# Queueing four kinds of loads behind the last tile's transposed exponentials in a two-layer decoder trunk

## The chip, the cores and the metric

One core of a Trainium2 chip runs the whole program. The metric is the device time of one execution in microseconds. PE is the matrix engine (TensorE), PEld its weight loads, DVE is VectorE, ACT is ScalarE, POOL is GpSimd, and SP is SyncE, whose queue issues every DMA of this kernel.

## The reference

Two layers of a decoder. The first is forgetting attention, the second a dilated sliding-window attention in three groups; both end in a gate and an output projection. The change touches only the first layer:

```python
def fox_mixer(h, w_in, b_f, q_g, k_g):
    proj = h @ w_in                                   # 1024 x 4112
    q = rms_norm(proj[..., :INNER]...); k = rms_norm(...); v = ...; gate = ...
    c = jnp.cumsum(jax.nn.log_sigmoid(f_logit), axis=1)
    o = fox_attention(q, k, v, c)     # softmax(q k / 8 + c_i - c_j, causal) v, 16 heads of 64
    return o.reshape(B, S, INNER), gate

x = x + (o * jax.nn.silu(gate)) @ w_out               # 1024 tokens, width 1024
```

## The kernel before, in words

Sequence and width are 1024 each. Products that need float32 accuracy run as three matmuls over a high and a low half of each operand. The heads are taken in eight pairs. For each pair a loop goes over eight tiles of 128 tokens: PE projects keys, queries and values of the tile (line 313, 24 matmuls), and between these matmuls PE works on the attention of pairs that were projected earlier. The classes and functions that matter:

- `Weights.load(i)` (line 253) brings quarter i of the next pair's raw weights, 384 KB, into one of two buffers called `raw`. `bound(i)` (line 258) reduces it on DVE to `vm`, and `split(k)` makes the high half on ACT (line 289) and the low half on POOL or DVE (line 291). A buffer is free when its two splits are done.
- `heads_tile`, `heads_sums` and `heads_pair` normalize the projected heads. ACT squares the projection into `sq` (line 383), DVE sums the squares (line 396) and scales (lines 398, 419, 420, 422), and the result is split into `hl` on ACT, POOL and DVE (lines 424 to 426). `turn()` (line 430) has a transposing DMA write two tiles' keys and queries to `qk_t`.
- `load_bc(hp, h, es)` (line 624) broadcasts half h of the cumulative forget sums of a head, 256 KB, to `bc`.
- `fox_tile(hp, t, ...)` is the attention of one tile of 128 queries. Its `score(e, c)` has PE make scores `s` in PSUM for head e of the pair (line 450, and the diagonal mask at line 656; three such PSUM buffers), and DVE adds `bc`, takes the running maximum and writes `p` (line 658), which frees the PSUM buffer. `p_transpose` then takes the exponential on ACT (line 492), splits it into the two halves of `ph` on ACT (line 495) and POOL (line 498), and one transposing DMA turns `ph` into `ptt` (line 499). There are two `ph` buffers, so a cast into `ph` waits until the transpose two places earlier has landed. `values(e)` has PE multiply `ptt` by the values `vt` (lines 506 to 508) into `o`; DVE divides (lines 688, 691), and the result goes to `y_d` (line 695). `gsf` (line 640) is the gate of the tile.

A counter called `Flow` runs four ticks per tile, and every step is queued at a tick. Tile 7's scores of a pair are due 57 and 59 ticks after the pair begins, and its values 67 and 69 ticks after. A pair takes 32 ticks, so while PE projects pair q it still finishes tile 7 of pair q-2. PE's own order is the written one. On the other engines and on the SP queue a scheduler decides the order at build time: it lets an instruction go ahead of one written earlier if it expects it to be ready sooner, and nothing but data and buffers holds it back. Each engine and the SP queue then take their instructions strictly in that order.

Of the kernel before, what the change touches and what calls it, by code (L numbers as in the profile page):

```python
# [2 lines left out]

# [1 line left out]

# [17 lines left out]
P = 128  # L23
# [3 lines left out]
NT = S // P  # L27
NH = 16
HD = 64
NHP = NH // 2  # L30
# [52 lines left out]
def trunk(ctx, tc, ins, out, cfg):  # L83
    nc = tc.nc
# [20 lines left out]
    flow = Flow()  # L105

    layer = {}

    def next_layer(bufs):
        if layer:  # L110
# [16 lines left out]
    c_d = dram.tile([NH, S], F32, name="c_d")  # L127
# [110 lines left out]
    class Weights:  # L238
# [9 lines left out]
        def load(self, i, tag=None):  # L248
            if tag is None:
                self.raw[i] = w_p.tile([P, 2, 384], F32, name="raw", tag="raw", bufs=2)  # L250
            else:
                self.raw[i] = lay([P, 2, 384], F32, name="raw", tag=tag)
            nc.sync.dma_start(self.raw[i][:, :, : self.n], self.src[:, 2 * i : 2 * i + 2, :])

        def bound(self, i):
            if self.vcols is None:
# [230 lines left out]
    def p_transpose(ne, nk, exps, splits):  # L487

        ph = lay([P, ne, 2, nk], F16, name="ph", tag="ph")
        pt = lay([P, ne * 2 * nk // P, P], F16, name="ptt", tag="ptt")  # L490
        for p, acc in exps:
            nc.scalar.activation(p, p, AF.Exp, bias=acc, scale=-1.0)  # L492
        for e, cols, p, pool_l in splits:
            if cfg["ph"]:
                nc.scalar.copy(ph[:, e, 0, cols], p)  # L495
            else:
                nc.vector.tensor_copy(ph[:, e, 0, cols], p)
            (nc.gpsimd if pool_l else nc.vector).tensor_sub(ph[:, e, 1, cols], p, ph[:, e, 0, cols])  # L498
        nc.sync.dma_start_transpose(pt, ph.rearrange("p e a k -> p (e a k)"))
        return pt.rearrange("p (e a k) s -> p e a k s", a=2, e=ne)  # L500

    def pv(o, e, blocks, vt):
# [116 lines left out]
    bcs = {}  # L619

    def load_bc(hp, h, es=(0, 1)):
        for e in es:
            bcs[hp, e, h] = lay([P, 512], F32, name="bc", tag="ga")
            nc.sync.dma_start(bcs[hp, e, h], c_d[2 * hp + e, h * 512 : (h + 1) * 512].partition_broadcast(P))

    def fox_tile(hp, t, kts, vt, sl):
        LP = cfg["lpf"]
        nk = (t + 1) * P
        st = {}
        pieces = [(a, min(a + 512, nk)) for a in range(0, nk, 512)]  # L630
        both = len(pieces) == 1
        accs = {}
        ptl = {}
        ps = {0: [], 1: []}

        def score(e, c):
            a, b = pieces[c]
            if e == 0 and c == 0:
                gs = st["gs"] = lay([P, P], F32, name="gsf", tag="gsl")
                nc.sync.dma_start(gs, gs_d[t * P : (t + 1) * P, hp * P : (hp + 1) * P])  # L640
            if c == 0:
                accs[e] = BIG
                st["acc"] = sm.tile([P, 2], F32, name="acc", tag="acc", bufs=8)
            if t < 2:
                if e == 0:
                    st["p"] = lay([P, 2, nk], F32, name="p", tag="p")
                p = st["p"][:, e]
            else:
                p = lay([P, b - a], F32, name="p", tag="p")
            ps[e].append(p)  # L650
            s = ps_s.tile([P, 512], F32, name="s", tag="s")
            runs = [(kts[j // 2], j % 2, n) for j, n in key_runs(range(a // P, b // P))]
            scores(s, kts[t // 2], t % 2, e, runs, b < nk)
            if b == nk:

                nc.tensor.matmul(s[:, t * P - a : b - a], ident_b, tri_b, start=False, stop=True, skip_group_check=True)
            acc = st["acc"][:, c : c + 1]
            nc.vector.tensor_tensor_reduce(p, s[:, : b - a], bcs[hp, e, a // 512][:, : b - a], -1.0, accs[e], ALU.add, ALU.min, acc)  # L658
            accs[e] = acc
            pl = (cfg["pl"] & 1, cfg["pl"] >> 1 & 1)  # L660
            if c < len(pieces) - 1 or both and e == 0:
                return
            if both:
                exps = [(ps[i][0], accs[i]) for i in range(2)]
                if t < 2:
                    splits = [(slice(0, 2), slice(0, nk), st["p"], pl[1])]
                else:
                    splits = [(i, slice(0, nk), ps[i][0], pl[i]) for i in range(2)]
                pt = p_transpose(2, nk, exps, splits)
                for i in range(2):  # L670
                    ptl[i] = [(pt[:, i, 0, j], pt[:, i, 1, j], j) for j in range(t + 1)]
            else:
                exps = [(p, accs[e]) for p in ps[e]]
                splits = [(0, slice(*pieces[i]), ps[e][i], pl[i]) for i in range(2)]
                pt = p_transpose(1, nk, exps, splits)
                ptl[e] = [(pt[:, 0, 0, j], pt[:, 0, 1, j], j) for j in range(t + 1)]

        def values(e):
            if e == 0:
                st["o"] = ps_o.tile([P, 2, HD + 1], F32, name="o", tag="o")  # L680
            pv(st["o"], e, ptl[e], vt)
            if e == 1:
                finish()

        def finish():
            o = st["o"]
            rec = sm.tile([P, 2], F32, name="rec", tag="rec")
            nc.vector.reciprocal(rec, o[:, :, HD])
            y = sb.tile([P, P], F32, name="y", tag="y")
            for e in range(2):  # L690
                nc.vector.scalar_tensor_tensor(y[:, e * HD : (e + 1) * HD], o[:, e, :HD], rec[:, e : e + 1], st["gs"][:, e * HD : (e + 1) * HD], ALU.mult, ALU.mult)
            if hp == NHP - 1:
                turn_last(y, t, flow.now + 3)
            else:
                nc.sync.dma_start(y_d[t * P : (t + 1) * P, hp * P : (hp + 1) * P], y)


        ts, tv = cfg["fox"][both]
        for e in range(2):
            for c in range(len(pieces)):  # L700
                urgent(lambda e=e, c=c: score(e, c), "ps", sl + ts[e * len(pieces) + c])
            urgent(lambda e=e: values(e), "pv", sl + LP + tv[e])
# [29 lines left out]
    for hp in range(NHP):  # L732
        w2 = (fox_weights(hp + 1) if hp + 1 < NHP else part(w_fo, 0)).ahead()
        s0 = flow.now
        if hp == 0:
            load_bc(0, 0)
# [3 lines left out]
        kts = []  # L740
# [3 lines left out]
        for t in range(NT):  # L744
# [4 lines left out]
            if t % 2:  # L749
                with tc.high_priority(cfg["ph_"]):  # L750

                    turn = heads_pair(0, t - 1, hd)
                    flow.at(flow.now + (6 if hp < NHP - 1 else 4), lambda turn=turn, kts=kts: kts.append(turn()))
                for i in range(2):

                    tt = t - 1 + i
                    fox_tile(hp, tt, kts, vt, s0 + (cfg["due"][tt] if hp < NHP - 1 else 4 * tt + 18))
            if hp == NHP - 1:

                a = max(flow.now + 1, s0 + cfg["due"][t] - 4 * NT + cfg["lpf"] + 9)  # L760
# [350 lines left out]
```

## Time and profile before

| what | value |
|---|---|
| median of 3 runs | 1816.11 us (1810.0 to 1819.2) |
| the profiled execution | 1818.5 us, its span 1816.7 us |
| mean granted PE clock | 0.99 |
| PE, PEld busy | 1737.0 us (96%), 1641.7 us (90%) |
| DVE, ACT, POOL busy | 1093.3, 1011.0, 973.5 us |
| DMA queue of SP | 288.36 MB, 71.4% of the 16 engines' span |

The times in the views are microseconds from the start of the span. The first layer's attention over the pairs lies between about 110 and 590 us; pairs 2 to 7 begin near 193, 247, 302, 357, 412 and 467 us. A matmul's busy time includes its latency, so a busy PE is not a PE at its peak; an idle PE, on the other hand, is a loss wherever nothing else makes up for it.

### The profile page before, as it was taken

The page shows a single profiled execution, that of the slowest core. Times are in us where ns is not written, and L with a number is a line of the kernel's source. Part 1 is how long each engine was busy: PE and PEld are TensorE (multiplying, and loading weights), DVE is VectorE, ACT ScalarE, POOL GpSimd, SP SyncE. Part 2 cuts the span into 40 slices and gives each one's busy share as a digit, 9 for nine tenths or more (in the row PEclk, how much of TensorE's full clock was granted, in tenths as well). Part 3 has the DMA queues.
Part 4 walks back from the last instruction along what each step waited for, and adds up shares of the span by engine and source line. Part 5 has one row for each costly group of instructions (what it writes and reads, how often), then busy time and mean ns, then how long its engine had stood idle before and what let it go on. Part 6 is the DMA issues. An engine that isn't in the chain of part 4 may idle for free.

```text
span 1816.7 us, 38150 instructions
## 1 busy us (share of the span) xinstructions
PE 1737.0 (96%) x13276; PEld 1641.7 (90%) x13276; DVE 1093.3 (60%) x3674; ACT 1011.0 (56%) x2696; POOL 973.5 (54%) x1175
## 2 busy tenths in 40 slices
PE   7999999999988989999999999999999999999999
PEld 6999888888876779999999989999999999999877
DVE  8546666666664453365556585666675666667631
ACT  6536666666665465455555665555555555555620
POOL 4215565556545431255656566667576666757530
PEclk9999999999999999999999999999999999999999
DMA  8447999999999763456767687667677776667852
GB/s 285 127 130 140 193 190 185 176 177 183 187 190 207 213 188 114 127 113 134 142 133 144 146 191 143 157 140 152 138 163 144 162 151 143 149 140 179 189 154 85
DMA packets 653189, 290.79 MB, mean 160 GB/s; under 512 B 512306, under 2 KB 616754, under 8 KB 652996
## 3 DMA queue, kind: packets, MB, share of 16 engines
q1 hardware_dynamic: 652996, 288.36, 71.4%
q8 instruction: 104, 1.70, 0.4%
q14 instruction: 89, 0.73, 0.1%
HBM read 126.46 MB, written 37.03 MB: 90 GB/s over the span
## 4 chain that ended last, share of the span: by engine, by line
PE 45%; DMA 12%; DVE 6%; ACT 4%; issue 3%; POOL 3%; SPq 1%; DVEq 0%; POOLq 0%; ACTq 0%
PE pj L313 33%; PE pj L336 7%; DMA raw<-in_w_dsw 5%; PE s L450 2%; DMA qk_t<-hl 2%; DMA ptt<-ph 2%; DMA og_d<-og 1%; POOL hl L425 1%; POOL w L291 1%; DMA cmb<-og_d 1%; DVE w L291 1%; DVE hl L426 1%; DVE u L422 1%; PE ob L506 1%; DVE p L906 1%
## 5 line engine op out<-in xcount | busy, mean ns | idle before, releaser
L313 PE MATMUL pj<-w,xh 128*128 128x384 f32 (+2 forms) x4864 | 1259.6, 341 | 30.2 <-ACT w L289 7.3
L313 PEld LDWEIGHTS pj<-w,xh 128*128 128x128 f32 x4864 | 873.1, 191 | 38.9 <-DVE ge L481 7.8
L313 PE MATMUL pj<-w,xl 128*128 128x384 f32 (+2 forms) x2432 | 817.6, 336 | 0.2 <-DVE xl L530 0.2
L313 PEld LDWEIGHTS pj<-w,xl 128*128 128x128 f32 x2432 | 464.7, 191 | 0.9 <-DVE xl L530 0.9
L291 POOL TENSOR_TENSOR w<-raw,w 128x384 fp32r<-128x384 f32 (+2 forms) x258 | 261.7, 1035 | 233.3 <-ACT w L289 228.8
L498 POOL TENSOR_TENSOR ph<-p,ph 128x512 f16<-128x512 f32 (+3 forms) x176 | 172.9, 999 | 161.9 <-ACT ph L495 160.7
L289 ACT CAST w<-raw 128x384 fp32r<-128x384 f32 (+2 forms) x352 | 162.6, 501 | 114.8 <-PE pj L336 37.4
L425 POOL TENSOR_TENSOR hl<-u,hl 128x512 f16<-128x512 f32 x128 | 151.2, 1181 | 125.0 <-ACT hl L424 124.9
L912 POOL TENSOR_TENSOR ph<-p,ph 128x768 f16<-128x768 f32 (+2 forms) x96 | 155.3, 1618 | 102.9 <-ACT ph L911 102.9
L383 ACT ACTIVATE sq<-pj 128x256 f32<-128x256 f32 x256 | 97.2, 380 | 168.9 <-DVE u L378 167.2
L450 PE MATMUL s<-qk_t 128*128 128x128 f16 (+1 forms) x1504 | 162.0, 248 | 19.2 <-DVE acc L658 10.4
L336 PE MATMUL pj<-xh,w 128*128 128x512 f32 x512 | 170.4, 404 | 2.2 <-ACT p L907 1.1
L258 DVE TENSOR_REDUCE vm<-raw 128x1 f32<-128x256 f32 x128 | 53.6, 419 | 156.2 <-DMA raw<-in_w_dsw 118.6
L506 PEld LDWEIGHTS <-ptt 128*128 128x128 f16 x1136 | 102.9, 98 | 48.8 <-issue 27.5
L389 DVE SCALAR_TENSOR_TENSOR vt<-pj,vsr,vt 128x128 f16<-128x128 f32 x256 | 89.6, 350 | 93.2 <-ACT vt L388 92.8
L450 PEld LDWEIGHTS <-qk_t 128*128 128x128 f16 x1504 | 110.2, 98 | 36.1 <-issue 22.0
L424 ACT CAST hl<-u 128x512 f16<-128x512 f32 x128 | 79.2, 619 | 104.9 <-DVE u L422 88.6
L495 ACT CAST ph<-p 128x512 f16<-128x512 f32 (+3 forms) x176 | 88.9, 537 | 72.7 <-DMA ptt<-ph 72.3
L492 ACT ACTIVATE p<-p,acc 128x512 f32<-128x512 f32 (+2 forms) x192 | 109.0, 609 | 30.6 <-DVE acc L658 27.4
L336 PEld LDWEIGHTS pj<-xh,w 128*128 128x128 f32 x512 | 97.6, 191 | 24.5 <-DVE xr L779 1.5
L378 DVE TENSOR_TENSOR u<-pj,gr 128x256 f32<-128x256 f32 x256 | 106.4, 416 | 18.4 <-PE pj L313 18.3
L907 ACT ACTIVATE p<-p,og 128x128 f32<-128x128 f32 (+1 forms) x256 | 98.1, 441 | 33.6 <-DVE og L906 33.4
(171 smaller groups left out, 2609.4 us busy)
## 6 DMA issues: line engine op xcount, KB each, us to landing
raw<-in_w_dsw SPq DMA_DIRECT2D x96, 384.0 KB, 3.7
raw<-in_w_fox SPq DMA_DIRECT2D x32, 384.0 KB, 3.7
og_d<-og SPq DMA_DIRECT2D x64, 132.0 KB, 3.2
cmb<-og_d SPq DMA_DIRECT2D x64, 132.0 KB, 3.3
bc<-c_d SPq DMA_DIRECT2D x32, 256.0 KB, 3.9
gs_d<-ge SPq DMA_DIRECT2D x32, 192.0 KB, 3.2
xt<-in_xt SPq DMA_DIRECT2D x16, 256.0 KB, 6.1
xrow<-in_x SPq DMA_DIRECT2D x8, 512.0 KB, 6.3
```

Source lines behind the costliest of these rows:

```text
L289: nc.scalar.copy(w[:, 0, :n], raw[:, k % 2, :n])
L291: eng.tensor_sub(w[:, 1, :n], raw[:, k % 2, :n], w[:, 0, :n].bitcast(F32))
L313: nc.tensor.matmul(ps[:, :n], a[:, k, cols], w.slabs[k][:, j, :n], start=(k == 0 and i == 0), stop=(k == KT - 1 and i == 2))
L336: nc.tensor.matmul(ps[m], w.slabs[k][:, j, m * P : (m + 1) * P], a[:, k, 512 * b : 512 * (b + 1)], start=(k == 0 and x == 0), stop=(k == K ...
L378: nc.vector.tensor_mul(u[:, t % 2].rearrange("p (a b) d -> p a b d", a=2), ps[:, : 4 * HD].rearrange("p (a b d) -> p a b d", a=2, b=2), gr ...
L425: nc.gpsimd.tensor_sub(hl[:, :, :4, 1], u, hl[:, :, :4, 0])
L450: nc.tensor.matmul(s[:, c0 : c0 + cnt * P].rearrange("p (c s) -> p c s", c=cnt), qk[:, i, blk], kk[:, j : j + cnt, e], start=(h == 0), sto ...
L492: nc.scalar.activation(p, p, AF.Exp, bias=acc, scale=-1.0)
L498: (nc.gpsimd if pool_l else nc.vector).tensor_sub(ph[:, e, 1, cols], p, ph[:, e, 0, cols])
L506: nc.tensor.matmul(o[:, e, :], hi, vt[:, j, e, HD:], start=(b == 0), stop=False, skip_group_check=True)
L907: nc.scalar.activation(p[:, e], p[:, e], AF.Exp, bias=acc[:, e : e + 1], scale=-1.0)
L912: nc.gpsimd.tensor_sub(ph[:, 1], st["p"], ph[:, 0])
```

## The change

A function `queued()` gives a context in which everything that is issued on SP is ordered behind one remembered instruction: the transposing DMA of tile 7's second head, of the pair that last traced it. The edge is one of issue order alone; nothing waits for that DMA to end. Three things are put in such a context: the loads of `bc` for the first half of the keys, the transposing DMA of tiles 6 and 7's keys, and quarter 0 of every raw weight load. No instruction is added or removed.

```diff
+    last = {}
+
+    def queued():
+        return tc.issue_after(last["late"]) if "late" in last else nullcontext()
...
         def load(self, i, tag=None):
...
-            nc.sync.dma_start(self.raw[i][:, :, : self.n], self.src[:, 2 * i : 2 * i + 2, :])
+            with queued() if i == 0 else nullcontext():
+                nc.sync.dma_start(self.raw[i][:, :, : self.n], self.src[:, 2 * i : 2 * i + 2, :])
...
     def p_transpose(ne, nk, exps, splits):
...
-        nc.sync.dma_start_transpose(pt, ph.rearrange("p e a k -> p (e a k)"))
+        last["ptt"] = nc.sync.dma_start_transpose(pt, ph.rearrange("p e a k -> p (e a k)")).ins
...
     def load_bc(hp, h, es=(0, 1)):
         for e in es:
             bcs[hp, e, h] = lay([P, 512], F32, name="bc", tag="ga")
-            nc.sync.dma_start(bcs[hp, e, h], c_d[2 * hp + e, h * 512 : (h + 1) * 512].partition_broadcast(P))
+            with queued() if h == 0 else nullcontext():
+                nc.sync.dma_start(bcs[hp, e, h], c_d[2 * hp + e, h * 512 : (h + 1) * 512].partition_broadcast(P))
...
     def fox_tile(hp, t, kts, vt, sl):
...
                 pt = p_transpose(1, nk, exps, splits)
+                if t == NT - 1 and e == 1:
+                    last["late"] = last["ptt"]
...
-                    flow.at(flow.now + (6 if hp < NHP - 1 else 4), lambda turn=turn, kts=kts: kts.append(turn()))
+
+                def turned_keys(turn=turn, kts=kts, t=t):
+                    with queued() if t == NT - 1 else nullcontext():
+                        kts.append(turn())
+
+                flow.at(flow.now + (6 if hp < NHP - 1 else 4), turned_keys)
```

The lines of the changed file are shifted by 6 to 14 (253 is 259, 258 is 264, 383 is 389, 430 is 436, 499 is 505, 624 is 631, 640 is 647, 658 is 665). PE's order is the same in both programs, row by row. The same pieces of order change once in each of the pairs 2 to 7, and in the tail of the layer; what follows is the place where pair 4 begins.

On SP, before. `ptt_4225` and `ptt_4286` are tile 7's two heads of pair 2, `ptt_4376` tile 0 of pair 3, `qk_t_4394` the keys of tiles 4 and 5, `bc_4605` and `bc_4846` the first-half sums of pair 4, `bc_5178` a second-half one, and `raw_4439`, `raw_4531`, `raw_4838` quarters 0 to 2 of pair 5's weights.

```order
L624 DMA bc_4605<-c_d_87 128x512
L624 DMA bc_4846<-c_d_87 128x512
L624 DMA bc_5178<-c_d_87 128x512
L430 DMA_TRANSPOSE qk_t_4394<-hl_4163 128x12x128
L695 DMA y_d_83<-y_4350 128x128
L499 DMA_TRANSPOSE ptt_4225<-ph_4224 128x16x128
L253 DMA raw_4439<-in_w_fox 128x768
L499 DMA_TRANSPOSE ptt_4286<-ph_4285 128x16x128
L499 DMA_TRANSPOSE ptt_4376<-ph_4375 128x4x128
L640 DMA gsf_4441<-gs_d_88 128x128
L253 DMA raw_4531<-in_w_fox 128x768
L253 DMA raw_4838<-in_w_fox 128x768
```

On SP, in the change, from the same row on:

```order
L436 DMA_TRANSPOSE qk_t_4394<-hl_4163 128x12x128
L704 DMA y_d_83<-y_4350 128x128
L505 DMA_TRANSPOSE ptt_4225<-ph_4224 128x16x128
L647 DMA gsf_4441<-gs_d_88 128x128
L505 DMA_TRANSPOSE ptt_4286<-ph_4285 128x16x128
L505 DMA_TRANSPOSE ptt_4376<-ph_4375 128x4x128
L259 DMA raw_4439<-in_w_fox 128x768
L259 DMA raw_4531<-in_w_fox 128x768
L631 DMA bc_4605<-c_d_87 128x512
L631 DMA bc_4846<-c_d_87 128x512
L505 DMA_TRANSPOSE ptt_4457<-ph_4456 128x8x128
L631 DMA bc_5178<-c_d_87 128x512
```

Three `bc` loads went from ahead of tile 7's transposes to behind them, and quarter 0 of the weights from between the two transposes to behind tile 0's. Quarter 2 (`raw_4838`) now comes four rows after the last one shown, behind the transposed keys of tiles 6 and 7 (`qk_t_4607`), which were behind tile 7's transposes already.

On DVE the scheduler follows. Before, from the normalization sums of pair 3's tiles 6 and 7 (`rs_v_4411`) on; `p_4503` and `p_4577` are the scores of tile 4's two heads of pair 3:

```order
L398 SCALAR_TENSOR_TENSOR rs_v_4411<-pj_4320,rx_124 128x8
L258 TENSOR_REDUCE vm_4426<-raw_4439 128x1
L389 SCALAR_TENSOR_TENSOR vt_3489<-pj_4320,vsr_3491,vt_3489 128x2x64
L658 ISA p_4503,acc_4502<-s_4504,bc_3666 128x512
L658 ISA acc_4502 128x1
L419 SCALAR_TENSOR_TENSOR pj_4320<-pj_4320,rs_v_4411 128x8
L658 ISA p_4510,acc_4502<-s_4511,bc_4239,acc_4502 128x128
L658 ISA acc_4502 128x1
L420 SCALAR_TENSOR_TENSOR pj_4320<-pj_4320,rs_y_4415 128x8
L378 TENSOR_TENSOR u_4533<-pj_4432,gr_109 128x256
```

On DVE, in the change:

```order
L395 SCALAR_TENSOR_TENSOR vt_3489<-pj_4320,vsr_3491,vt_3489 128x2x64
L425 SCALAR_TENSOR_TENSOR pj_4320<-pj_4320,rs_v_4411 128x8
L426 SCALAR_TENSOR_TENSOR pj_4320<-pj_4320,rs_y_4415 128x8
L665 ISA p_4503,acc_4502<-s_4504,bc_3666 128x512
L665 ISA acc_4502 128x1
L428 TENSOR_TENSOR u_4314<-u_4314,pj_4320 128x512
L665 ISA p_4510,acc_4502<-s_4511,bc_4239,acc_4502 128x128
L665 ISA acc_4502 128x1
L384 TENSOR_TENSOR u_4533<-pj_4432,gr_109 128x256
L264 TENSOR_REDUCE vm_4426<-raw_4439 128x1
L697 RECIPROCAL rec_4570<-o_4475 128x2
```

The reduction of quarter 0 (line 258, now 264) moved behind the scores of tile 4's first head and the scaling of those tiles (line 422, now 428). On the rows that follow in the change it stands ahead of the second head's scores (`p_4577`).

Some rows later on DVE, before: the sums of the squares of pair 4's tiles 0 and 1 (line 396), and the scores of tile 5's first head (`p_4691`).

```order
L378 TENSOR_TENSOR u_4533<-pj_4539,gr_109 128x256
L688 RECIPROCAL rec_4682<-o_4675 128x2
L691 SCALAR_TENSOR_TENSOR y_4684<-o_4675,rec_4682,gsf_4360 128x64
L396 TENSOR_REDUCE pj_4539<-sq_4534 128x8
L691 SCALAR_TENSOR_TENSOR y_4684<-o_4675,rec_4682,gsf_4360 128x64
L658 ISA p_4691,acc_4690<-s_4692,bc_3666 128x512
```

In the change:

```order
L697 RECIPROCAL rec_4682<-o_4675 128x2
L402 TENSOR_REDUCE pj_4539<-sq_4534 128x8
L700 SCALAR_TENSOR_TENSOR y_4684<-o_4675,rec_4682,gsf_4360 128x64 x2
L264 TENSOR_REDUCE vm_4426<-raw_4838 128x1
L404 SCALAR_TENSOR_TENSOR rs_v_4653<-pj_4539,rx_124 128x8
L665 ISA p_4691,acc_4690<-s_4692,bc_3666 128x512
```

Here the reduction of quarter 2 (`raw_4838`) came to stand ahead of `p_4691`; it used to stand ahead of the second piece of tile 4's second head. The squares `sq_4534` that line 396 needs moved as well. On ACT, before and then in the change, with `ph_4635` the halves of tile 2:

```order
L492 ACTIVATE p_4618<-p_4618,acc_4617 128x384
L492 ACTIVATE p_4627<-p_4627,acc_4626 128x384
L495 CAST ph_4635<-p_4618 128x384
L383 ACTIVATE sq_4534<-pj_4539 128x256
L495 CAST ph_4635<-p_4627 128x384
```

```order
L498 ACTIVATE p_4618<-p_4618,acc_4617 128x384
L389 ACTIVATE sq_4534<-pj_4539 128x256
L498 ACTIVATE p_4627<-p_4627,acc_4626 128x384
L422 ACTIVATE rs_y_4657<-rs_v_4653 128x8
L394 ACTIVATE vt_4428<-pj_4539,vsr_4430 128x2x64
L501 CAST ph_4635<-p_4618 128x384
```

The square now stands two rows ahead of the cast into `ph_4635`, behind which it stood.

More of the change, by code (lines that the diff above doesn't have):

```diff
@@ L1 @@
 import heapq
-from contextlib import ExitStack
+from contextlib import ExitStack, nullcontext
 import numpy as np
```

## The prediction

> **What bounds the kernel now.** I read first how busy each engine is in the pairs that the change touches, then what PE waits for there, then the queues of SP, DVE and ACT in one pair.
>
> ```profile
> 305.00:360.00 55.00, 51.14 (x502) 47.76 (x502) 35.03 (x127) 34.88 (x88) 31.93 (x32) 0.97 0.91 183
> 360.00:415.00 55.00, 51.46 (x511) 47.92 (x510) 35.40 (x127) 35.05 (x88) 32.73 (x34) 1.00 0.93 182
> 415.00:470.00 55.00, 50.73 (x500) 47.24 (x499) 35.36 (x127) 35.22 (x88) 32.20 (x32) 0.97 0.98 184
> ```
>
> The columns are the stretch and its length, PE, PEld, DVE, ACT and POOL busy, the granted clock, DMA share and GB/s. PE is busy for 51 of 55 us and no other engine for over 36, so PE sets the length of a pair and idles 3.5 to 4.3 us in each. What it waits for, over pairs 2 to 7 (186 to 510 us):
>
> ```profile
> PE o L506 <- DMA ptt<-ph: 13.2, 10, 2.9
> PE s L450 <- DVE acc L658: 10.0, 9, 2.0
> PE s L450 <- DMA qk_t<-hl: 1.2, 1, 1.2
> ```
>
> Total, times, longest. The chance of a gain lies in these 24.4 us. In the pair that begins at 357 us four waits stand, in order; then the second-head waits of pairs 2, 3 and 7:
>
> ```profile
> 362.75 0.20 PE L506 MATMUL o<-vt,ptt 128*128 128x65 f16 x1 [1.58 <-DMA ptt<-ph]
> 366.70 0.20 PE L506 MATMUL o<-vt,ptt 128*128 128x65 f16 x1 [0.31 <-DMA ptt<-ph]
> 371.78 0.38 PE L450 MATMUL s<-qk_t 128*128 128x256 f16 x2 [1.01 <-DVE acc L658]
> 378.62 0.38 PE L450 MATMUL s<-qk_t 128*128 128x256 f16 x2 [0.64 <-DVE acc L658]
> ...
> 202.41 0.20 PE L506 MATMUL o<-vt,ptt 128*128 128x65 f16 x1 [0.20 <-DMA ptt<-ph]
> 256.51 0.20 PE L506 MATMUL o<-vt,ptt 128*128 128x65 f16 x1 [0.22 <-DMA ptt<-ph]
> 477.76 0.20 PE L506 MATMUL o<-vt,ptt 128*128 128x65 f16 x1 [1.15 <-DMA ptt<-ph]
> ```
>
> The first of each pair is for tile 7's first head, the second for its second head. The four second-head waits are 0.20 + 0.22 + 0.31 + 1.15 = 1.9 us of the 13.2; the other six, 11.3 us, are first-head waits.
>
> **The first head gains nothing.** The SP queue of that pair:
>
> ```profile
> 352.13 1.33 SPq L624 DMA_DIRECT2D bc<-c_d  x3
> 355.65 1.43 SPq L430 DMA_TRANSPOSE qk_t<-hl  x1
> 357.18 1.09 SPq L695 DMA_DIRECT2D y_d<-y  x1
> 358.36 1.85 SPq L499 DMA_TRANSPOSE ptt<-ph  x1
> 360.31 1.04 SPq L253 DMA_DIRECT2D raw<-in_w_fox  x1
> 361.44 4.50 SPq L499 DMA_TRANSPOSE ptt<-ph  x2
> ...
> SPq L430 <- DVE hl L426: 2.1, 1, 2.1
> raw<-in_w_fox SPq DMA_DIRECT2D x32, 384.0 KB, 3.7
> bc<-c_d SPq DMA_DIRECT2D x32, 256.0 KB, 3.9
> ```
>
> The three `bc` issues end at 353.46, and then SP stands 2.1 us waiting for DVE's last piece of `hl` before it can issue the keys of tiles 4 and 5. These keys and `y_d` stay ahead of tile 7's first transpose. So the 1.33 us that leave this place come out of idle time, and I cost them at nothing; if `hl` came 2.1 us sooner they would show. As transfers, the last `bc`, issued near 353, lands by its usual 3.9 us near 357, when the keys' own transpose, issued at 355.65, is just beginning. I take zero; the bound is that all 11.3 us go.
>
> **The second head gains up to 2 us.** The 384 KB of quarter 0 leave the place between the two transposes. Their issue takes 1.04 us. From issue to PE's use, the first head takes 362.75 - 358.36 = 4.4 us and the second, behind the raw load, 366.70 - 361.44 = 5.3 us. So the second lands 0.4 us (a `gsf` is in its place, issued in some 0.5 us) to 1.9 us sooner, more than each of its waits but perhaps the 1.15: 1.4 to 1.9 us of the 1.9 us.
>
> **The waits for `acc`.** These are PSUM buffers that DVE has not yet freed. The queues of DVE and then ACT:
>
> ```profile
> 364.74 0.42 DVE L258 TENSOR_REDUCE vm<-raw 128x1 f32<-128x256 f32 x1 [3.30 <-DMA raw<-in_w_fox]
> 370.32 0.42 DVE L258 TENSOR_REDUCE vm<-raw 128x1 f32<-128x256 f32 x1 [1.06 <-DMA raw<-in_w_fox]
> 371.04 0.68 DVE L658 CUSTOM_DVE_ANT_0 p<-s,bc 128x512 f32<-128x512 f32 x1
> 377.08 0.69 DVE L396 TENSOR_REDUCE pj<-sq 128x8 f32<-128x512 f32 x1 [1.88 <-ACT sq L383]
> 377.88 0.68 DVE L658 CUSTOM_DVE_ANT_0 p<-s,bc 128x512 f32<-128x512 f32 x1
> ...
> 376.26 0.51 ACT L495 CAST ph<-p 128x384 f16<-128x384 f32 x1 [1.14 <-DMA ptt<-ph]
> 376.68 0.38 ACT L383 ACTIVATE sq<-pj 128x256 f32<-128x256 f32 x1
> ...
> DVE vm L258 <- DMA raw<-in_w_fox: 22.1, 12, 3.6
> ```
>
> PE's 371.78 is the end of the `p` begun at 371.04, which stood behind quarter 1's reduction; PE's 378.62 is the end of the `p` begun at 377.88, which stood behind a sum of squares, and this behind a cast on ACT that waited for a transpose to land. DVE loses 22.1 us in twelve such waits for raw weights. The change takes away the 3.30 at its place, puts the tile 4 scores and the key scaling there, and on ACT puts the square ahead of the waiting cast.
>
> Worked through for this pair: quarter 0 is now issued after tile 0's transpose, which ended at 365.94 and comes some 0.6 us sooner without the raw load ahead of it: near 365.3 instead of 360.31, and by its 3.7 us lands near 369.0. DVE meets its reduction near 367.2 (the work from 365.1 to 367.2 stood behind it before), so it waits 1.8 us there instead of 3.3. Then come the 0.42, a reciprocal, two `y` and a copy of `hl`, near 1.1 us, and tile 4's second head begins at 370.5 instead of 371.04: PE's wait of 1.01 shrinks by 0.5, having begun up to 0.3 earlier. Next, the square no longer waits for the transpose: the sum of squares moves from 377.08 to some 375. But quarter 2, issued behind the keys of tiles 6 and 7 near 372, lands at 375.7 by 3.7 us, or about 1 us later behind that transpose, and its reduction now stands ahead of the next `p`. That `p` starts at 376.3 to 377.3 rather than 377.88, 0.6 to 1.6 us sooner. PE's last release of the pair is what counts: the waits before it only move within it. I take 1.0 us, nearer the lower end because quarter 2 stands in a chain of three waits (POOL's splits, SP, DMA). The ends are below nothing, -0.7 (a wait of the 1.8 kind moves in front of `p`), and 2.0, all the three later waits of this pair.
>
> **What is late next.** Three transfers arrive later than before: the `bc`, needed only when the next pair's first tiles are scored, half a pair on; the raw quarters, 4 us later, whose splits have until the next pair's projection; and the first tile 4 transpose, behind quarter 2 and ACT's splits of quarter 0, about 1 us later. None of the ten waits for `ptt` is tile 4's, so I cost these at nothing; if the slack of tile 4 were under 1 us, it would cost 6 times the excess.
>
> **Two smaller terms.** A wait also slows the clock:
>
> ```profile
> 306.00:314.00 8.00, 5.74 (x65) 5.43 (x66) 3.03 (x13) 4.51 (x14) 3.78 (x4) 0.79 0.91 201
> 417.00:425.00 8.00, 7.18 (x78) 6.72 (x79) 3.35 (x12) 6.08 (x17) 4.50 (x5) 0.79 0.93 228
> 488.00:494.00 6.00, 4.15 (x18) 4.02 (x18) 4.84 (x17) 4.55 (x14) 3.36 (x4) 0.72 0.50 135
> ```
>
> Each holds a loss of 0.21 x 8 or 0.28 x 6 = 1.7 us of clock, right behind the waits near 305, 415 and 488 us. The third follows an `acc` wait, which the change shortens: half a chance, 0.85 us. The Trainium skill, TensorE: Matmul & The Clock Gate, Part 1, has the clock halved after an idle window of about 3.4 us and whole again after a busy one; by it no wait here is long enough to halve it, and without this term the sum would be 7.8 us. The trace differs: the longest of these waits is 2.9 us, and the losses are there.
>
> In the layer's tail the chain that ended last reads:
>
> ```profile
> 546.00 1.26 POOL w L291 x2
> 547.26 5.72 DMA ptt<-ph
> ```
>
> The two splits there are of the first raw quarter of the output weights, which the change puts behind the transpose. At most 1.26 us go, at worst none; I take 0.6.
>
> **The sum.** Six pairs at 1.0, pair 7's own second-head wait 1.15, the clock 0.85, the tail 0.6: 8.6 us. Against the profiled execution's 1818.5 us that is 1809.9; this execution is 2.4 us above the median of 1816.1, so 1807.5 there, 0.47% less. About 0.5% (9.1 us) is what a measurement of this kernel can tell from no change.
>
> **Rivals.** First, faster still: the first head's transpose comes sooner too, because less is in flight ahead of it. For it speaks that `bc` and keys meet near 357; against it, SP's 2.1 us wait for `hl`. With half of 11.3 us and one clock loss, 8.6 + 5.7 + 1.7 = 16 us: 1800.
>
> Second, nothing: the DMA engines bind, with shares of 0.91 to 0.98, and an order of the same bytes changes no sum; each PE wait only moves to the next transpose. Against it, nine of PE's 20 waits end with DVE, and 182 GB/s here stand beside 228 in the row from 417 us. It gives 1816, give or take 3. The Trainium skill, Perfetto Trace Analysis, What "DMA-bound" means, would say so if single DMA engines were full, though its section on the most-contended engine warns that the occupancy of 16 engines misleads.
>
> Third, slower: quarter 2's reduction blocks the `p` behind it. It decides from a landing later than 377.3 - here that is an issue later than 373.6, 1.6 us behind my estimate. With the 3.6 us of the longest wait for raw in front of `p`, the release comes up to 2 us later than now: six times 2 less pair 7's gain, 11 us: 1827.
>
> **Chances.** The forecast, a gain of 4 to 13 us, 0.60: 0.28 of it over 0.5%, 0.32 within. The first rival 0.12, all faster. Nothing 0.18, all within. Slower 0.10: 0.08 over 0.5%. That gives faster 0.40, same 0.52, slower 0.08. The forecast alone reaches from 1803 to 1812; with the first rival's likelier half and nothing, 1798 to 1820.
>
> **What would show it.** In the profile after: second-head waits on `ptt` gone, so ten waits become about six with some 11 us; the `acc` waits down from 10.0 us to about 5; DVE's 22.1 us for raw weights under 15; first-head waits unchanged near 1.3 to 2.9 us. If the first-head waits shrink, the first step is wrong; if the `acc` waits stay, quarter 2 took the place of the cast; if new waits on tile 4's `ptt` appear, its slack was misjudged.

## The result, and the profile after

The changed kernel is slower: 1820.49 us against 1814.78 us, medians of 20 runs each. The ratio is 1.0029, with a 95% interval of 1.0020 to 1.0037, so 3.6 to 6.7 us are lost (5.7 by the medians) where 8.6 were forecast as a gain. The profiled execution of the change has a span of 1817.3 us and a granted clock of 0.987, the one before 1816.7 us and 0.990. These two executions differ by far less than the medians do, so a single trace shows what waits for what, and the ratios say what it costs.

The three middle pairs, by the same windows as before (length, PE, PEld, DVE, ACT and POOL busy, clock, DMA share, GB/s):

```profile
305.00:360.00 55.00, 50.17 (x505) 46.79 (x504) 35.23 (x126) 34.45 (x88) 31.50 (x32) 1.00 0.89 180
360.00:415.00 55.00, 52.08 (x508) 48.75 (x507) 35.52 (x126) 35.09 (x89) 32.39 (x33) 0.97 0.93 183
415.00:470.00 55.00, 51.41 (x503) 48.02 (x502) 36.00 (x127) 35.60 (x89) 32.84 (x33) 0.97 0.96 190
```

PE still sets the length, and it idles 2.9 to 4.8 us of each 55, against 3.5 to 4.3 before. What it waits for over 186 to 510 us (total, times, longest), and DVE's largest waits there:

```profile
PE s L456 <- DVE acc L665: 10.9, 8, 2.0
PE o L512 <- DMA ptt<-ph: 10.0, 6, 2.1
PE pt L352 <- DVE acc L665: 2.6, 1, 2.6
...
DVE vt L395 <- ACT vt L394: 28.5, 14, 4.3
DVE vm L264 <- DMA raw<-in_w_fox: 21.1, 15, 2.6
DVE pj L402 <- ACT sq L389: 16.1, 19, 2.6
```

Ten waits for `ptt` became six, the first heads' alone. But PE's waits for `acc` went from 10.0 to 13.5 us (in a second profiled execution of each kernel, from 9.9 to 17.0). On DVE the waits for the square (29.5 before) fell to 16.1, those for raw weights stayed at 21.1, and those of `vt` for ACT grew from 17.5 to 28.5. In the pair that begins at 357.6 us, first SP's queue, then DVE's, then PE:

```profile
365.96 1.01 SPq L259 DMA_DIRECT2D raw<-in_w_fox  x2
367.02 0.90 SPq L631 DMA_DIRECT2D bc<-c_d  x2
...
371.40 2.02 SPq L436 DMA_TRANSPOSE qk_t<-hl  x1
373.52 0.53 SPq L259 DMA_DIRECT2D raw<-in_w_fox  x1
374.15 1.26 SPq L505 DMA_TRANSPOSE ptt<-ph  x1
...
369.46 0.42 DVE L264 TENSOR_REDUCE vm<-raw 128x1 f32<-128x256 f32 x1 [1.47 <-DMA raw<-in_w_fox]
371.14 0.68 DVE L665 CUSTOM_DVE_ANT_0 p<-s,bc 128x512 f32<-128x512 f32 x1
375.47 0.68 DVE L402 TENSOR_REDUCE pj<-sq 128x8 f32<-128x512 f32 x1
378.28 0.42 DVE L264 TENSOR_REDUCE vm<-raw 128x1 f32<-128x256 f32 x1 [1.76 <-DMA raw<-in_w_fox]
378.69 0.68 DVE L665 CUSTOM_DVE_ANT_0 p<-s,bc 128x512 f32<-128x512 f32 x1
...
379.43 0.38 PE L456 MATMUL s<-qk_t 128*128 128x256 f16 x2 [0.78 <-DVE acc L665]
```

The sum of squares now stands at 375.47 and waits for nothing, as forecast. The next row with a wait is the third quarter's reduction at 378.28. Its load was issued at 373.52, behind the keys, and was waited for until 378.28: 4.8 us from issue. It is 4.7 to 4.9 us in the same pair of four other profiled executions with that wait, and 4.8 also in the one of them where the keys are issued behind the quarter, so it takes no keys ahead of it to make it that long. The `p` of tile 5's first head stands behind it and starts at 378.69. The change has exchanged one wait in front of this `p` (1.88 us for ACT) for another (1.76 us for the quarter).

### The profile page after: what moved, and what is told of

It reads as the page before. It is cut to its first block, busy times and chain, and to the rows that moved or that the text cites. A ratio compares the mean times of both kernels' runs of the same rounds, so it can differ in the third digit from the quotient of the medians.

```text
span 1817.3 us, 38140 instructions
## 1 busy us (share of the span) xinstructions
PE 1739.6 (96%) x13276; PEld 1644.3 (90%) x13276; DVE 1093.1 (60%) x3674; ACT 1010.9 (56%) x2696; POOL 974.3 (54%) x1175
## 4 chain that ended last, share of the span: by engine, by line
PE 53%; DMA 19%; DVE 10%; ACT 7%; POOL 5%; issue 5%; SPq 1%; POOLq 0%; DVEq 0%; ACTq 0%
PE pj L319 40%; PE pj L342 6%; DMA ptt<-ph 6%; DMA raw<-in_w_dsw 4%; PE s L456 3%; POOL ph L504 2%; DMA qk_t<-hl 2%; DMA raw<-in_w_fox 2%; POOL hl L431 1%; POOL w L297 1%; ACT p L498 1%; DMA og_d<-og 1%; ACT ph L501 1%; DVE p L665 1%; DMA cmb<-og_d 1%
## 5 line engine op out<-in xcount | busy, mean ns | idle before, releaser
L456 PE MATMUL s<-qk_t 128*128 128x128 f16 (+1 forms) x1504 | 163.0, 249 | 21.9 <-DVE acc L665 11.9
L432 DVE COPY hl<-hl 128x512 f16<-128x512 f16 x128 | 69.5, 543 | 80.8 <-POOL hl L431 80.6
```

The lines of the kernel that those rows point to most:

```text
L456: nc.tensor.matmul(s[:, c0 : c0 + cnt * P].rearrange("p (c s) -> p c s", c=cnt), qk[:, i, blk], kk[:, j : j + cnt, e], start=(h == 0), sto ...
```

## The experiments

A ratio below is to the kernel before, run on the same chip. Intervals are 95%. The first theory was that the late third quarter, whose reduction stands ahead of `p`, is the loss; the second that the moved loads crowd the DMA engines; the third that all of it is scatter.

**The parts alone.** Queueing the keys by itself does nothing: with only that edit the program is that of the kernel before, and without it that of the change. The other two parts were run apart.

```diff
 # raw quarter alone: the other two contexts are empty
-    with queued() if h == 0 else nullcontext():   # load_bc
+    with nullcontext():
-    with queued() if t == NT - 1 else nullcontext():   # keys
+    with nullcontext():
```

> Only the first raw quarter is queued behind tile 7's second transpose; the forget sums and the keys are queued as before. Theory 1 (the third quarter of the weights, which waits for the buffer of the first, lands about 6 us later, and its reduction on DVE stands ahead of tile 5's first p): the late quarter is here, so PE's waits for acc in pairs 2 to 7 are 9 us or more, the reduction waits over 1 us for raw right before that p, and the time is that of the whole change, ratio 1.002 to 1.004. Theory 2 (the forget sums crowd the DMA engines where tile 7's transposes have left them): ratio 1.000 or a little under, 0.998 to 1.001, since the sums stay where they were. Theory 3 (it is the halved clock and the scatter of a reshuffled schedule, no one wait): anything from 0.998 to 1.004, with no tie to the acc waits.

Measured: 1.0030 (1.0019 to 1.0042), as much as the whole change loses. DVE in the pair that begins at 360.4 us:

```profile
380.56 0.42 DVE L264 TENSOR_REDUCE vm<-raw 128x1 f32<-128x256 f32 x1 [2.72 <-DMA raw<-in_w_fox]
...
381.94 0.68 DVE L665 CUSTOM_DVE_ANT_0 p<-s,bc 128x512 f32<-128x512 f32 x1
```

The wait for the quarter is there, 1.8 to 2.7 us in all five pairs 2 to 6, with about 1 us of other work between it and `p`. No second-head wait is left in pairs 2 to 7.

```diff
 # sums alone: the raw quarter and the keys as before
-    with queued() if i == 0 else nullcontext():   # Weights.load
+    with nullcontext():
```

> Only the loads of the forget sums (bc of the first half) are queued behind tile 7's second transpose; the first raw quarter goes where it went. Theory 1: quarter 0 is early, so its buffer comes free early and the third quarter is at most 2 us later than in the kernel before; PE's waits for acc stay near 10 us; tile 7's transposes lose the three sums ahead of them, up to 1 us per pair; ratio 0.997 to 1.000. Theory 2: the loss is the sums', ratio 1.002 to 1.004. Theory 3: 0.998 to 1.004.

Measured: 1.0007 (0.9994 to 1.0020), not told from no change, where the second theory had 1.002 to 1.004. The second-head waits stay; the first and second heads of the pair that begins at 358.5 us:

```profile
363.99 0.20 PE L512 MATMUL o<-vt,ptt 128*128 128x65 f16 x1 [2.04 <-DMA ptt<-ph]
367.88 0.20 PE L512 MATMUL o<-vt,ptt 128*128 128x65 f16 x1 [0.24 <-DMA ptt<-ph]
```

So moving the raw quarter out from between the two transposes is what ends the second head's wait, and the raw quarter's later place is what loses the time.

**The reduction behind `p`.** The changed kernel, with one order added on DVE. The order on SP, PE and POOL stays as it was; on DVE the reduction and a few rows beside it move, and on ACT one row in each of five pairs.

```diff
 # bound(i), third quarter; p5 is the first p of tile 5's first head
-    nc.vector.tensor_reduce(self.vm[:, i : i + 1], ...)
+    with tc.issue_after(last["p5"]) if i == 2 and "p5" in last else nullcontext():
+        nc.vector.tensor_reduce(self.vm[:, i : i + 1], ...)
```

> The whole change, and besides it the third quarter's reduction (L264) is put behind the first p of tile 5's first head on DVE, so that a late quarter can't hold that p. SP's queue is that of the changed kernel. Theory 1: the second wait for acc of each pair (1.3 to 1.9 us) falls under 0.5, the sum of PE's waits for acc in pairs 2 to 7 from 10.9 + 2.6 to under 8 us, and the ratio from 1.0029 to between 0.997 and 1.001. Theory 2: the transposes of tile 7 and of the keys are as late as in the changed kernel, and so is the rest: ratio 1.002 to 1.004, with the lost time moved from acc to ptt or qk_t. Theory 3: no change beyond 0.001 either way.

Measured: 1.0003 (0.9991 to 1.0015). DVE in the pair that begins at 357.2 us, then PE's waits over 186 to 510 us:

```profile
374.64 0.68 DVE L402 TENSOR_REDUCE pj<-sq 128x8 f32<-128x512 f32 x1
...
376.57 0.68 DVE L665 CUSTOM_DVE_ANT_0 p<-s,bc 128x512 f32<-128x512 f32 x1
377.17 0.08 DVE L665 DVE_READ_ACCUMULATOR2_ANT acc<- 128x1 f32 x1
377.51 0.42 DVE L264 TENSOR_REDUCE vm<-raw 128x1 f32<-128x256 f32 x1 [0.26 <-DMA raw<-in_w_fox]
...
PE o L512 <- DMA ptt<-ph: 13.3, 6, 2.9
PE s L456 <- DVE acc L665: 5.0, 6, 1.3
PE pt L352 <- DVE acc L665: 2.1, 1, 2.1
```

`p` starts at 376.57, within the forecast's 376.3 to 377.3 and before the quarter has landed, and the waits for `acc` of 13.5 us are down to 7.1. From the start of pair 2 to that of pair 7 this kernel took 270.3 us, and 269.6 in a second profiled execution, where the two of the change took 274.1 and 275.8. The same edit on the kernel before tells whether it is a gain by itself:

> The kernel before, with the third quarter's reduction put behind the first p of tile 5's first head and nothing of the change. It tells whether that edit is a gain of its own or only mends what the change broke. Theory 1 (the late quarter is the change's loss): in the kernel before the third quarter is reduced 6 us ahead of that p, at 371.65 against 377.88, and the p is held by the reduction of squares, which waits for ACT; so the edit frees nothing: ratio 0.998 to 1.001, and PE's waits for acc in pairs 2 to 7 stay at 9 to 11 us. Rival: the edit is worth 0.26% anywhere, and the loss of the change has another cause: ratio 0.996 to 0.998, with PE's waits for acc under 7 us.

Measured: 0.9997 (0.9981 to 1.0014). There the edit is worth nothing. DVE waits for the square ahead of that `p` (2.46 us in this kernel's same pair), whatever the reduction does. PE's waits for `acc` are 7.5 us, under the 9 to 11 that were expected, and the time did not follow them. So the edit mends what the change broke. The opposite edit, the kernel before with the third quarter late:

```diff
 # base: the kernel before; keys is the transpose of tiles 6 and 7's keys
+    with tc.issue_after(last["keys"]) if i == 2 and "keys" in last else nullcontext():
         nc.sync.dma_start(self.raw[i][:, :, : self.n], ...)
```

> The kernel before, with nothing of the change but this: the third raw quarter is queued behind the transpose of tiles 6 and 7's keys, as the change's order happens to have it. Theory 1: the late quarter alone costs what the change lost, ratio 1.002 to 1.005, and a wait for raw over 1 us stands ahead of a p of tile 5 on DVE, unless the scheduler puts the reduction behind that p, in which case the waits for acc stay at 10 us and the ratio at 1.000. Theory 2: no sums are moved, ratio 0.999 to 1.001. Theory 3: 0.998 to 1.004.

Measured: 1.0015 (1.0004 to 1.0027), half of the loss. The scheduler put the reduction behind tile 5's `p` in four of the five pairs; in pair 2 it stands ahead of another `p` and waits 1.61 us, and PE waits 1.86 us for that. The experiment is weaker than meant, and where its loss lies is not shown.

With the keys behind tile 4's first transpose, SP issues the third quarter ahead of the keys:

```diff
-    with queued() if t == NT - 1 else nullcontext():   # keys
+    with tc.issue_after(last["t4"]) if t == NT - 1 and "t4" in last else nullcontext():
```

> The changed kernel, but the keys of tiles 6 and 7 are queued behind tile 4's first transpose rather than behind tile 7's second. SP then issues the third quarter and tile 4's first transpose ahead of the keys. Theory 1b: the quarter lands about 2 us sooner and its reduction no longer stands right before tile 5's p (the wait for raw there under 0.5 us), the cast that waits for tile 4's transpose goes 2 us sooner, and the last pair is back at 124 to 126.2 us: ratio 0.998 to 1.001. Theory 2 (the sums and quarters crowd the DMA engines wherever the keys stand): ratio 1.002 to 1.004.

> The same, and the third quarter's reduction behind tile 5's first p as well. Theory 1b: with the late quarter already mended by the queue the second edit adds little: ratio within 0.001 of the kernel with the keys behind tile 4's transpose alone, 0.997 to 1.000. If instead it is lower by 0.002 or more, the reduction's place on DVE is what counts and not the queue's.

Measured: 1.0025 (1.0008 to 1.0043), where 0.998 to 1.001 was expected, and 1.0004 (0.9987 to 1.0020) with the reduction behind `p`. DVE in the first of the two, in the same pair:

```profile
376.14 0.42 DVE L264 TENSOR_REDUCE vm<-raw 128x1 f32<-128x256 f32 x1 [2.30 <-DMA raw<-in_w_fox]
...
377.60 0.68 DVE L665 CUSTOM_DVE_ANT_0 p<-s,bc 128x512 f32<-128x512 f32 x1
```

The quarter came 2 us sooner, and the scheduler put its reduction earlier by as much: the wait stayed, at 1.8 to 2.3 us in the five pairs (1.8 to 2.5 in the change). What counts is the place of the reduction on DVE against its load, not the load's time alone. In each of these kernels with a ratio of 1.0025 and over, that wait stands in front of tile 5's `p` in all five pairs. One thing does not fit: in the pair shown `p` starts no later than in the kernel before (377.88), PE's waits for `acc` are 7.0 us in all, less than the 10.0 before, and the five pairs took 272.5 us, against 274.2 and 273.6. Its trace does not show where it loses, and only the two ratios, 1.0025 and 1.0004, tell what the reduction's place costs there.

**Both kernels once more.** The changed kernel and the one before:

> The changed kernel once more, beside the others on this chip. All theories: ratio 1.002 to 1.004 as on the first chip. Theory 1 asks for more in the trace: a wait of DVE for raw of 1.2 us or more right ahead of tile 5's first p in at least four of the five pairs 2 to 6. Theory 3 (scatter of the halved clock) would have the time from pair 2 to pair 7 within 1 us of the kernel before in this look too (274.1 against 274.3 us in the first two), and all of the loss elsewhere.

> The kernel before, one more look, to have the scatter of one execution: from pair 2 to pair 7 it took 274.3 us in the first profile, in an execution 3.7 us above its median. Theory 1: this one lies under that, by 2 to 5 us; theory 3: at 274.3 within 1 us.

Measured: 1.0028 (1.0013 to 1.0042) for the change, with the wait of 1.85 to 2.7 us in front of `p` in all five pairs. From pair 2's start to pair 7's the two profiled executions of the kernel before took 274.2 and 273.6 us, those of the change 274.1 and 275.8: 1 us apart in the mean. The first theory had asked for a second execution of the kernel before that is 2 to 5 us under the first; that missed. From pair 7's start to the last tile's reciprocal they took 126.3 and 124.5 against 127.5 and 128.4, 2.6 us more. That was not in the first theory, which puts the loss into pairs 2 to 6.

**The last pair.** No raw weights are reduced in it, but its queue differs by one load, the first quarter of the output projection's weights. (The first raw quarter is thus queued for two kinds of weights; with the sums and the keys these are the four kinds of the title.) In the second execution of the change, SP, ACT, DVE and PE in turn:

```profile
485.08 2.04 SPq L436 DMA_TRANSPOSE qk_t<-hl  x1
487.22 0.53 SPq L259 DMA_DIRECT2D raw<-in_w_fo  x1
487.85 1.26 SPq L505 DMA_TRANSPOSE ptt<-ph  x1
...
494.21 0.51 ACT L501 CAST ph<-p 128x384 f16<-128x384 f32 x1 [4.73 <-DMA ptt<-ph]
...
495.53 0.35 DVE L395 SCALAR_TENSOR_TENSOR vt<-pj,vsr,vt 128x128 f16<-128x128 f32 x1 [4.23 <-ACT vt L394]
495.80 0.47 DVE L665 CUSTOM_DVE_ANT_0 p<-s,bc,acc 128x256 f32<-128x256 f32 x1
...
496.34 1.12 PE L352 MATMUL pt<-ident,yt 128*128 128x128 f32 x4 [3.45 <-DVE acc L665]
```

The chain: tile 4's first transpose is issued at 487.85, behind the keys and a quarter. The cast into tile 2's `ph` needs a buffer that this transpose frees, and waits 4.73 us. ACT's `vt` stands behind the cast, DVE's `vt` behind ACT's, the second `p` of tile 5 behind DVE's, and PE waits 3.45 us (2.60 in the first execution). Two edits take that one load apart:

```diff
 # the kernel before, with the last pair's quarter queued (vcols is None for the output projection)
+    with queued() if i == 0 and self.vcols is None else nullcontext():
         nc.sync.dma_start(self.raw[i][:, :, : self.n], ...)
```

```diff
 # the change without the last pair's quarter (vcols is set for FoX weights)
-    with queued() if i == 0 else nullcontext():
+    with queued() if i == 0 and self.vcols is not None else nullcontext():
```

> The kernel before, with one edit: the first raw quarter of the output projection's weights, which is loaded in the last pair alone, is queued behind tile 7's second transpose. Theory 1b (besides the late quarter, the change loses in the last pair: tile 4's first transpose now stands behind the keys of tiles 6 and 7 on SP, ACT's cast of the next ph waits for its landing, ACT's vt stands behind that cast, DVE's vt behind ACT's, and the second p of tile 5 behind DVE's vt): from pair 7's start to the last tile's reciprocal 127 to 128.5 us, against 124.5 to 126.2 in three kernels without the edit; a wait of DVE for ACT's vt of 3.5 us or more before 500 us; ratio 1.0008 to 1.0025. Rival (the 3 us in the last pair are scatter, and the pairs 2 to 6 hold the loss): 124.5 to 126.2 us, ratio 0.9992 to 1.0006.

> The changed kernel, but the first quarter of the output projection's weights goes where it went before, so only the last pair differs from the changed kernel. Theory 1 (the third quarter's reduction, which stands in front of tile 5's first p in pairs 2 to 6, is the loss): it still waits 1.5 to 2.7 us for raw there in all five pairs, ratio 1.001 to 1.004, within 0.001 of the changed kernel's 1.0028. Theory 1b (the last pair holds half of the loss): 1.000 to 1.0015.

> The whole change with the third quarter's reduction behind tile 5's first p, but the first quarter of the output projection's weights goes where it went in the kernel before, so the last pair has its old queue. Theory 1b: the last pair takes 124 to 126.2 us, pairs 2 to 7 271 to 273 us, ratio 0.997 to 0.9995, the first version under the kernel before. Rival (the last pair is scatter): as the whole change with the reduction behind, 0.9991 to 1.0015.

> The version that came out at 0.9981, once more: the whole change without the output projection's quarter, and the third quarter's reduction behind tile 5's first p. If it beats the kernel before, 0.997 to 0.9995 again; if that was scatter of the comparison, 0.9995 to 1.001.

> The whole change with the third quarter's reduction behind tile 5's first p, once more and on the chip of the two above, so that the last pair's part is read from kernels side by side. Theory 1 without 1b: within 0.001 of the version without the output projection's quarter. Theory 1b: 0.0015 or more above it; 0.9995 to 1.0015 either way.

```
                                           ratio (95%)
quarter queued in the last pair only       0.9999 (0.9984 to 1.0015)
change                                     1.0029 (1.0020 to 1.0037), 1.0028 (1.0013 to 1.0042)
change without the last pair's quarter     1.0007 (0.9991 to 1.0023)
change, reduction behind p                 1.0003 (0.9991 to 1.0015), 1.0005 (0.9989 to 1.0022)
both of the last two edits                 0.9981 (0.9968 to 0.9995), 0.9981 (0.9965 to 0.9998)
```

Call the last two edits mends. Each is worth 0.2 to 0.3%, with or without the other: the reduction's 1.0029 to 1.0003 and 1.0007 to 0.9981 (and 1.0025 to 1.0004 with the keys behind tile 4's transpose), the last pair's 1.0029 to 1.0007 and 1.0003 to 0.9981. (The intervals of two such rows can touch; what carries it is that each step came out more than once.) The change without the last pair's quarter still has the wait of 1.8 to 2.8 us in front of `p` in all five pairs, so the first theory's expectation for it, 1.0028 within 0.001, missed: that wait is about half of what was lost. With both mends the kernel is faster than the one before, in two measurements on two chips, by 0.0019 x 1815 = 3.4 us.

A second expectation missed: the quarter queued in the last pair alone cost nothing. The last pair's wait for `acc`, in the kernel before (second execution), with that quarter queued alone, and in the change with the reduction behind:

```profile
490.44 0.38 PE L450 MATMUL s<-qk_t 128*128 128x256 f16 x2 [1.96 <-DVE acc L658]
```

```profile
492.13 0.66 PE L352 MATMUL pt<-ident,yt 128*128 128x128 f32 x4 [2.05 <-DVE acc L665]
```

```profile
490.42 0.66 PE L352 MATMUL pt<-ident,yt 128*128 128x128 f32 x4 [2.12 <-DVE acc L665]
```

On the kernel before, the queued quarter replaces a wait of 1.96 us, for the square, by one of 2.05 us, for `vt`: no loss. With both mends the first kind and the second are gone. SP and DVE there:

```profile
480.93 2.51 SPq L505 DMA_TRANSPOSE ptt<-ph  x1
483.53 1.35 SPq L436 DMA_TRANSPOSE qk_t<-hl  x1
484.97 1.47 SPq L259 DMA_DIRECT2D raw<-in_w_fo  x1
...
488.22 0.48 DVE L665 CUSTOM_DVE_ANT_0 p<-s,bc,acc 128x256 f32<-128x256 f32 x1
```

Tile 4's transpose is ahead of the keys again, and PE waits for no `acc` there: 2.1 us less. The change without that quarter has the same queue there and waits 1.88 us for `acc`, so the queue alone does not decide this wait. And other waits lengthen in these executions. From pair 7's start to the last reciprocal the two executions took 125.4 and 125.1 us with the quarter queued, and 125.6 and 125.0 without; the change without that quarter took 127.0, close to the change's 127.5 and 128.4.

The kernels with the keys behind tile 4's transpose speak against the chain too. There tile 4's transpose is ahead of the keys in the last pair as well, and PE's wait is short:

```profile
490.77 0.66 PE L352 MATMUL pt<-ident,yt 128*128 128x128 f32 x4 [0.70 <-DVE acc L665]
```

Yet this stretch took 127.2 us there, and 128.4 with the reduction behind `p`, where 124 to 126.2 was expected, and with the reduction behind the ratio is 1.0004 and not 0.9981. (That edit moves the keys in all six pairs, so it is no clean test.) So the last pair's edit is worth 0.2% by the ratios, the chain of waits is in the traces, and that the chain is its cause is not shown. Where the 4 us lie stays open; single executions scatter by some microseconds, and there are one or two of each kernel.

**The sums' share.**

> The queued forget sums alone, with the third quarter's reduction behind tile 5's first p; the first raw quarter goes where it went in the kernel before. Theory 1: the first quarter costs nothing where it was, and the third is not late by much, so this is as good as the whole change with the reduction behind: ratio 0.997 to 1.001. Rival (the gain of the whole change with that edit comes from the first quarter's later place, which clears the way for tile 7's second transpose): ratio 1.000 to 1.003, and the second-head waits of 0.2 to 0.6 us per pair stay.

> Of the change only the first raw quarter of the FoX weights, and the third quarter's reduction behind tile 5's first p; the forget sums go where they went. If the sums' later place is worth something once the reduction is out of the way, this lies 0.001 or more above the version with the sums moved; if the sums don't matter, within 0.0007 of it, 0.998 to 1.000; if they cost (as 1.0022 for the sums with the reduction behind suggests), below it.

Measured: the sums with the reduction behind `p` 1.0022 (1.0007 to 1.0036), above the 0.997 to 1.001 that the first theory gave. The rival's second-head waits are there (0.26 to 0.66 us in five pairs), and so is the wait for the square (2.84 us in front of tile 5's `p`). But both stand in the kernel before as well, and neither the late quarter nor the last pair's load is in this one: what loses its 0.2% is not shown. The FoX raw quarter with the reduction behind, sums as before, gave 0.9989 (0.9973 to 1.0004), beside 0.9981 with the sums moved. The 0.0008 between these lies inside both intervals: whether the sums' place matters stays open.

## Why the prediction was wrong

**First head.** Held. Six first-head waits stay, 10.0 us in the first execution and 11.9 in the second, against 11.3 before.

**Second head.** Held in its waits: none is left in either execution of the change. That they go with SP's raw load between the transposes is shown by the two parts run alone.

**The waits for `acc`.** This step failed. Up to the square it went as worked through: the first quarter was waited for 1.47 us (forecast 1.8) until 369.46 (forecast 369.0), and the square was out of the way at 375.47 (375). The term that was mis-sized is the landing of quarter 2: issued at 373.52 where I had put 372, and waited for until 378.28 where I had put 375.7 to 376.7. I had added at most 1 us to the median landing of 3.7, and it was 4.8 us here. This is past the point that the third rival names, a landing later than 377.3, though the issue was not past the 373.6 that it derives from it. Why this load takes longer than the median is not shown; the transpose of the keys, for which I had allowed 1 us, is not needed for it, since the quarter took 4.8 us without it too. I gave that rival 0.10, though my own margin to it was 0.6 us at the near end. What the wait costs is 0.0026 x 1815 = 4.7 us over five pairs by the ratios with and without it, 0.9 us each, less than the rival's 2. The lengths from pair 2's start to pair 7's agree: 5 us less in the mean with the reduction behind. And the gain was there to be lost: with the reduction out of the way `p` starts at 376.57, where the forecast had it, and the pairs take 270 us against the 273.9 of the kernel before, 0.8 us less each where I took 1.0. The missing piece was that on DVE, which takes its rows in the order of the program, the reduction had to move along with its load.

**What is late next.** Half of it failed. I costed tile 4's first transpose at nothing because no PE wait was tile 4's. PE never did wait for it. But the transpose also frees a `ph` buffer, and ACT's cast waits for that: 4.73 us in the last pair, passed on through three queues to PE. The slack had to be asked for every user of the buffer, not for the tile's own consumer alone. Putting the last pair's queue back is worth 0.2% by the runs; that this chain is the reason is not shown.

**The smaller terms.** Not gained. The clock loses in four stretches of the FoX pairs in the first execution of the change and in two in the second, against three and one before (last section). The wait for `ptt` near 592 us is 3.64 us, before 3.58, so the tail's 0.6 us is not there. I also took 0.5% for the least that can be told from no change; 20 runs of each told 0.29%.

**Nothing, and faster.** The second rival's ground, full DMA engines, is not what decided: shares of 0.91 to 0.93 go with 0.9981 and 0.89 to 0.96 with 1.0029, over the same three windows, and what differs is where a reduction and one load stand. The first rival's shorter first-head waits did not come. The gain that the forecast looked for is there but smaller: 3.4 us (0.4 to 6.4, from the widest ends of the two intervals) with both mends, not 8.6. PE's waits for `acc` are down there from 10.0 and 9.9 us to 7.1 and 4.1, but the first heads wait 12.1 and 13.9 us, against 11.3 and 12.1 before: a part may have moved to the next transpose, as the second rival had it. From pair 2's start to pair 7's the two executions of that version took 271.3 and 272.3 us, 2.1 less in the mean than the kernel before; the starts stand first and last in this row of the second one, for ACT's `vsr`:

```profile
L752 ACT ACTIVATE vsr<-rx,vs x6: 287/288/292, 193.0 to 465.3; 128x8 f32<-128x8 f32 x6
```

## What to carry to other kernels

When a load is queued later, follow its buffer: the load that reuses the buffer is late too, and on an engine that works in order the instruction that reads it may now stand in front of the one that everybody waits for. Move the reader along with the load, or put an order between it and the critical instruction; here the later load alone lost time, the order alone did nothing, and together they cost nothing and, with the last pair's load left where it was, brought a little. Ask also which buffer each delayed transfer frees, and what stands behind the instruction that waits for that buffer.

## What the runs showed of the hardware

The granted clock again fell after waits of PE of about 2 us. Two first-head waits in the first execution of the change, and three stretches, behind these two and behind the wait of 2.60 us that ended at 492.86:

```profile
363.45 0.20 PE L512 MATMUL o<-vt,ptt 128*128 128x65 f16 x1 [2.14 <-DMA ptt<-ph]
473.71 0.23 PE L512 MATMUL o<-vt,ptt 128*128 128x65 f16 x1 [1.89 <-DMA ptt<-ph]
```

```profile
362.00:370.00 8.00, 6.55 (x75) 6.25 (x76) 3.05 (x12) 5.04 (x15) 2.96 (x3) 0.79 0.91 215
472.00:480.00 8.00, 6.29 (x72) 5.84 (x73) 2.87 (x11) 4.77 (x14) 3.01 (x3) 0.79 0.81 194
492.00:500.00 8.00, 7.14 (x60) 6.21 (x60) 6.05 (x21) 6.43 (x16) 4.17 (x6) 0.79 0.57 131
```

Each is a loss of 0.21 x 8 = 1.7 us. A fourth stretch, 418 to 426 us, has 0.79 as well, behind a first-head wait of 2.02 us. The Trainium skill, TensorE: Matmul & The Clock Gate, Part 1, has the clock halved after an idle window of about 3.4 us. The trace differs: the waits here are 1.89 to 2.60 us, and PE was busy for 1.3 us of the 3.4 us that end at 363.4. That the wait is the reason is read from the order in time alone. Not every such wait is followed by a loss: the second execution of the change has a first-head wait of 2.81 us, up to 419.7 us, and a clock of 1.00 behind it. So a single execution can lose 1.7 us more or less than the next.
